# A convolution's running sum moved to PSUM, and two heads' outputs in one staging tile, in a hybrid decoder trunk

## The chip, the cores and the metric

One core of one Trainium2 chip runs the whole program. The metric is the device time of one execution in microseconds.

## The reference, cut to what matters

The program computes DEPTH = 2 layers on x of 1024 tokens by 1024 channels, all in float32:

```python
h = rms_norm(x);  proj = h @ w_in            # one projection, split over three branches
# A) y = a * sigmoid(a_glu); causal depthwise convolution with 31 taps over tokens, 256 channels;
#    layer norm, silu, 256x256 product; times silu(z_conv)
# B) latent attention: 8 heads, key width 96, value width 64, causal softmax in blocks of 128
#    queries; times silu(z_mla)
# C) chunked spatial gating, 256 channels; times silu(z_sg)
x = x + concat(rms_norm(yA), rms_norm(yB), rms_norm(yC)) @ w_out
```

## The kernel before

Every float32 product is made from operands that are split in two parts (a rounded high part and the low rest, both of type fp32r), so a product is two or three matmuls. The high part is a copy on ScalarE (ACT), the low part a subtraction on VectorE (DVE) or GpSimd (POOL). TensorE (PE) has its own order of work, written as a long sequence of units.

A layer runs so. First come the projection units V, A0, A1, U, ZS, ZC, ZM0 and ZM1, eight row tiles or two halves of channels each. A0 and A1 are the two blocks of 128 channels of the convolution branch. When one is projected, its gated input stands in an SBUF tile `yp` (128 channels by 30 + 1024 tokens), and a function `tap(j)` is queued 31 times: tap 0 is a `tensor_scalar` (line 514), taps 1 to 30 are `scalar_tensor_tensor` instructions (line 517), each of which multiplies 1024 shifted columns of `yp` with one weight per channel and adds the running sum `acc`, in place, all in SBUF. The taps of both blocks are handed out as filler work for DVE, 1.45 us apart by the planner's clock (`flow.add_fill`), beside what the projection units ask of DVE: `silu2` (line 549) for ZS, ZC and ZM, `mix` (line 541), and the norm of the gating branch (lines 560 and 565). Behind the taps, four `conv_norm` steps are queued, which transpose `acc` on PE into the bank `ct` (line 596), and from there the branch goes on through `conv_swish` and `conv_point`, all between the matmuls of ZM0 and ZM1. POOL meanwhile makes low parts of weights (line 213) and the products of the gating branch (line 576).

PSUM has eight banks: four of tag `b1` (one bank each, for nearly every output) and two tiles of tag `b2` (two banks each, function `bank2`). The tiles of `b2` hold transposes of the layer's input (`pth`, `pty`) and the scores of attention; nothing asks for one between the end of unit V and the attention.

Attention goes over 8 heads with an order that a greedy planner makes from estimated times: scores (`score`), transposes of the probabilities (`ptrans`), products with the values (`pv`), and `finish`. The values of a head are split by `v_split` into a tile `vh` with the 64 high columns beside the 64 low ones, so one product with the transposed probabilities gives 128 rows, 64 of the high part and 64 of the low. The two are added into a tile `os` of 64 rows by 512 queries (an ACT copy, line 1097, then a DVE addition, line 1098). `finish` transposes `os` back in four pieces of 64 by 128 into a bank `ot` and multiplies the result into the gate tile `zsm` (line 1106). This happens for each head and each half of the queries, 16 times a layer.

The helper `mm` is line 154, every transpose (`tr`) is line 165, and a `split` is lines 169 and 170.

Of the kernel before, what the change touches and what calls it, by code (L numbers as in the profile page):

```python
# [10 lines left out]
F32 = mybir.dt.float32  # L11
# [3 lines left out]
ALU = mybir.AluOpType  # L15
# [4 lines left out]
P = 128  # L20
S = 1024
# [5 lines left out]
TAPS = 31  # L27
# [4 lines left out]
DV = 64  # L32
# [31 lines left out]
for _name, _parts in UNITS:  # L64
# [10 lines left out]
PC_CW, PC_CB, PC_LG, PC_LB, PC_SB, PC_QN, PC_KVN, PC_QG, PC_KG = (  # L75
    0, 62, 64, 66, 68, 72, 78, 80, 81)
# [50 lines left out]
def hybrid_trunk(ctx, tc, x, w, pc, pr, sgw, pww, cst, out):  # L127
    nc = tc.nc
    flow = Flow()

    def open_pool(name, side, bufs=1, **kw):
        cm = tc.tile_pool(name=name, bufs=bufs, side=side, reuse_waits="tile", **kw)
        return cm, cm.__enter__()
# [9 lines left out]
    def bank(name):  # L143
        return ps.tile([P, 512], F32, tag="b1", bufs=4, name=name)
# [218 lines left out]
    for l in range(L):  # L363
# [34 lines left out]
        def chan(un, c0, half, final, name):  # L398

            flow.step()  # L400
            o = bank(name)
            t = hT[half]
            for k in range(KC):
                wh, wl = un.get(k)
                mm3(o, (wh[:, c0:c0 + P], wl[:, c0:c0 + P]), (t[:, 0, k, :], t[:, 1, k, :]),
                    k == 0, k == KC - 1)
                un.used(k, final)
            return o
# [82 lines left out]
        pcs, rg, bgr, dpc = cs  # L491
# [4 lines left out]
        for ct in (0, 1):  # L496
            yp = ap_.tile([P, TAPS - 1 + S], F32, tag="yp", bufs=2, name=f"yp{l}_{ct}")
            nc.gpsimd.memset(yp[:, :TAPS - 1], 0.0)
            un = Unit(l, f"A{ct}")
            for half in (0, 1):  # L500
                g_ps = chan(un, 128, half, False, f"glu{l}_{ct}{half}")
                tg = ap_.tile([P, 512], F32, tag="e2k", bufs=5 - l, name="tg")
                nc.scalar.activation(tg, g_ps, AF.Tanh, scale=0.5)
                a_ps = chan(un, 0, half, half == 1, f"a{l}_{ct}{half}")
                c0 = TAPS - 1 + half * 512
                nc.vector.scalar_tensor_tensor(out=yp[:, c0:c0 + 512], in0=tg, scalar=1.0, in1=a_ps,
                                               op0=ALU.add, op1=ALU.mult)
            acc = ap_.tile([P, S], F32, tag="acc", bufs=2, name=f"acc{l}_{ct}")
            accs.append(acc)

            def tap(j, ct=ct, yp=yp, acc=acc):
                wc = dpc[:, ct * TAPS + j:ct * TAPS + j + 1]
                if j == 0:
                    nc.vector.tensor_scalar(acc, yp[:, 0:S], wc, pcs[:, PC_CB + ct:PC_CB + ct + 1],
                                            op0=ALU.mult, op1=ALU.add)
                else:
                    nc.vector.scalar_tensor_tensor(out=acc, in0=yp[:, j:j + S], scalar=wc, in1=acc,  # L517
                                                   op0=ALU.mult, op1=ALU.add)
            flow.add_fill(1.45, [lambda j=j, f=tap: f(j) for j in range(TAPS)])

# [129 lines left out]
        zsm = cp.tile([P, NT, MW], F32, tag="zsm", name=f"zsm{l}")  # L650
# [6 lines left out]
        for i in range(NT):  # L657
            o = bank(f"pzk{l}_{i}")
# [66 lines left out]
        for half in (0, 1):  # L725
            acc = c2pool.tile([P, 512], F32, tag="sqa", bufs=2, name="sqkv")
            for c in (0, 1):
                o = chan(un, c * P, half, half == 1 and c == 1, f"ckv{l}_{c}{half}")
# [4 lines left out]
        for u in range(3):  # L733
            un = Unit(l, f"CQ{u}")
            for half in (0, 1):
                for c in (0, 1):
                    o = chan(un, c * P, half, half == 1 and c == 1, f"cq{l}_{u}{c}{half}")
# [55 lines left out]
        t1_cm, t1p = open_pool(f"T1_{l}", "left")  # L793
# [74 lines left out]
        def open_t():  # L868
# [3 lines left out]
            t_cm.append(cm)  # L872
            return tp
        attention(nc, flow, t1p, open_t, late_splits, [lambda i=i: query(1, i) for i in range(2, NT)],
                  bank, bank2, mm, mm3, tr, split, split_gain, ident_b, mask_b,
                  ksb, qsb, vsb, zsm, dpc[:DQK, 66:67], (early_load, early_norm), l)
# [101 lines left out]
def attention(nc, flow, t1p, open_t, late_splits, extra, bank, bank2, mm, mm3, tr, split, split_gain, ident_b, mask_b,  # L978
# [1 line left out]

    heads, probs, outs, vhs = {}, {}, {}, {}
    busy = {"act": flow.t, "dve": flow.t}
    LAG = 0.1
    SL_K, SL_S, SL_T, SL_P = 0.0, 0.0, 0.0, 0.0
# [7 lines left out]
    def est(eng, dur, ready):  # L994
        busy[eng] = max(busy[eng], ready + LAG) + dur
        return busy[eng]
# [5 lines left out]
    def v_split(h):  # L1002
        vh = vhs[h] = pool["t"].tile([P, NT, 2, DV], F32R, tag="vh", bufs=2, name=f"vh{l}_{h}")
        hc = vsb[:, :, h * DV:(h + 1) * DV]
        nc.scalar.copy(vh[:, :, 0, :], hc)
        nc.vector.tensor_tensor(out=vh[:, :, 1, :], in0=hc, in1=vh[:, :, 0, :].bitcast(F32),
                                op=ALU.subtract)
        est("dve", 0.6, est("act", 0.55, flow.t))

# [52 lines left out]
    def ptrans(h, half, j):  # L1062
        st = probs[h, half]
        off = max(0, j - 4 * half)
        pt = bank(f"pt{l}_{h}{half}{j}")
        for t in range(off, 4):
            tr(pt[:, t * P:(t + 1) * P], st[t][:, j * P:(j + 1) * P])
        tk = slice(off * P, 512)
        if j == 0:
            sm = st["sum"]  # L1070
            nc.vector.reciprocal(sm[:, 2, :], sm[:, 0, :])  # L1071
            z = zsm[:, half * 4:half * 4 + 4, h * DV:(h + 1) * DV]
            nc.gpsimd.tensor_tensor(out=z, in0=z, in1=sm[:, 2, :].unsqueeze(2).broadcast_to([P, 4, DV]),  # L1073
                                    op=ALU.mult)
        pT = pool["t"].tile([P, 2, 512], F32R, tag="pT", bufs=3, name=f"pT{l}_{h}{half}{j}")
        split(pT[:, 0, tk], pT[:, 1, tk], pt[:, tk])
        n = 512 - off * P
        fh = est("act", n / 1200 + 0.06, flow.t)
        fl = est("dve", n / 960 + 0.08, fh)
        b1_free.remove(min(b1_free))  # L1080
        b1_free.append(fl)
        return pT, tk, max(fh, fl - 0.2)

    def pv(h, half, j, pT, tk):
        nj = 4 * half + 4
        if j == 0:
            outs[h, half] = bank(f"o{l}_{h}{half}")
        o = outs[h, half]
        vv = vhs[h][:, j].rearrange("p a d -> p (a d)")
        mm(o[:, tk], vv, pT[:, 0, tk], j == 0, False)  # L1090
        mm(o[:, tk], vv, pT[:, 1, tk], False, j == nj - 1)
        pt_free.remove(min(pt_free))
        pt_free.append(flow.t)
        if j < nj - 1:
            return None
        os_ = t1p.tile([DV, 512], F32, tag="os", bufs=2, name="os")
        nc.scalar.copy(os_, o[DV:2 * DV, :])
        nc.vector.tensor_tensor(out=os_, in0=o[0:DV, :], in1=os_, op=ALU.add)
        return os_, est("dve", 0.7, est("act", 0.5, flow.t))

    def finish(h, half, os_):
        b = bank(f"ot{l}_{h}{half}")
        for t in range(4):
            tr(b[:, t * DV:(t + 1) * DV], os_[:, t * P:(t + 1) * P])
        z = zsm[:, half * 4:half * 4 + 4, h * DV:(h + 1) * DV]
        nc.vector.tensor_tensor(out=z, in0=b[:, 0:4 * DV].rearrange("p (t d) -> p t d", d=DV), in1=z,
                                op=ALU.mult)
        f = est("dve", 0.35, flow.t)
        b1_free.remove(min(b1_free))
        b1_free.append(f)  # L1110

# [65 lines left out]
    while sq or tq or pq:  # L1177
# [9 lines left out]
        if prio == 3:  # L1187
# [3 lines left out]
            if not x_left:  # L1191
                pool["t"] = open_t()
                v_split(0)
        elif prio == PRIO[0]:
            kind, h, i = sq.pop(0)
            if kind == "load":
                early_load(h)
            elif kind == "s":
                score(h, i)
            elif kind == "v":  # L1200
                v_split(h)
            elif kind == "w":
                splits = splits or late_splits()
                next(splits, None)
            else:
                qk_part(h, kind, i)
        elif prio == PRIO[2]:
            h, half, j = tq.pop(0)
            pT, tk, f = ptrans(h, half, j)
# [3 lines left out]
        else:  # L1213
            _, kind, h, half, *rest = pq.pop(0)
            if kind == "pv":
                j, pT, tk = rest
# [91 lines left out]
```

## Time and profile before

| what | us |
|---|---|
| median of three runs (1318.74, 1319.68, 1321.02) | 1319.68 |
| the profiled execution | 1318.69 |
| its span, first to last instruction | 1316.9 |
| PE busy in the span | 1258.1 |
| DVE busy | 835.6 |
| ACT busy | 532.4 |
| POOL busy | 431.4 |

The profiled execution has 1.8 us around its span, and stands at the lower end of the three runs. Times in the rows below count from the start of the span. Layer 0 has its convolution from about 67 to 220 us and its attention from about 404 to 570 us; layer 1 has the same at about 717 to 870 and 1053 to 1218 us. A busy PE is not PE at its peak, since matmuls are pipelined and a stall inside a queue of matmuls can be shown as busy.

### The profile page before, as it was taken

What the parts mean: (1) busy time and instruction counts of PE and PEld (TensorE: products, weight loads), DVE (VectorE), ACT (ScalarE), POOL (GpSimd) and SP (SyncE); (2) the same over time, 40 slices, a digit from 0 to 9 for tenths busy, and PEclk for the clock granted to TensorE, in tenths of its full rate; (3) what the DMA queues carried; (4) which work ended last, traced back from release to release, by engine and by line L of the source; (5) the groups of instructions that cost most, each with busy time, mean ns of one, the idle gap of its engine ahead of it and who ended that gap; (6) DMA issues with size and microseconds to landing.
All of it is one profiled execution on the core that took longest, in us unless ns stands there. A gap on an engine that the chain in (4) does not pass through costs nothing.

```text
span 1316.9 us, 19326 instructions
## 1 busy us (share of the span) xinstructions
PE 1258.1 (96%) x7566; PEld 1099.6 (84%) x7566; DVE 835.6 (63%) x1337; ACT 532.4 (40%) x1083; POOL 431.4 (33%) x388
## 2 busy tenths in 40 slices
PE   8999969999998999999999997899999989998998
PEld 7889969888996777778898997898889967777886
DVE  7499975114767888763454999631247788887431
ACT  6311324323435777740342122332243477776200
POOL 4733624534573000010046255334436710000100
PEclk9999979999998999999999999899999999999999
DMA  7121212212111000044432112011111100001333
GB/s 284 49 64 33 69 33 65 67 32 72 49 33 33 1 1 1 17 141 125 151 125 64 33 41 92 21 61 48 52 53 49 46 20 1 1 1 29 100 105 104
DMA packets 33820, 77.88 MB, mean 59 GB/s; under 512 B 3777, under 2 KB 12353, under 8 KB 33729
## 3 DMA queue, kind: packets, MB, share of 16 engines
q1 hardware_dynamic: 33728, 76.64, 18.6%
q8 instruction: 60, 0.98, 0.3%
q14 instruction: 32, 0.25, 0.1%
HBM read 64.05 MB, written 12.58 MB: 58 GB/s over the span
## 4 chain that ended last, share of the span: by engine, by line
PE 69%; DVE 21%; ACT 4%; issue 3%; POOL 1%; DMA 0%; SPq 0%; ACTq 0%; DVEq 0%; POOLq 0%
PE po L154 14%; DVE acc L517 13%; PE cq L154 10%; PE s L154 8%; PE qps L154 7%; PE o L154 5%; PE ckv L154 3%; PE pt L165 3%; PE pzk L154 3%; PE ZM L154 3%; PE V L154 2%; PE kps L154 2%; PE vps L154 2%; PE glu L154 2%; PE a L154 2%
## 5 line engine op out<-in xcount | busy, mean ns | idle before, releaser
L213 POOL TENSOR_TENSOR w<-raw,w 128x1024 fp32r<-128x1024 f32 (+1 forms) x49 | 137.2, 2809 | 150.1 <-ACT w L210 96.4
L154 PE MATMUL po<-w,yT 128*128 128x512 f32 x768 | 184.2, 398 | 0.0
L517 DVE SCALAR_TENSOR_TENSOR acc<-yp,dpc,acc 128x1024 f32<-128x1024 f32 x120 | 183.1, 1552 | 1.4
L154 PEld LDWEIGHTS po<-w,yT 128*128 128x128 f32 x768 | 143.0, 188 | 33.3
L154 PE MATMUL s<-kT,qT 96*128 96x384 f32 (+5 forms) x576 | 133.1, 358 | 3.7 <-ACT p L1053 3.7
L154 PE MATMUL o<-pT,vh 128*128 128x512 f32 (+3 forms) x384 | 129.8, 396 | 6.8 <-DVE pT L170 5.6
L154 PE MATMUL cq<-hT,w 128*128 128x512 f32 x576 | 131.9, 390 | 0.0
L154 PEld LDWEIGHTS cq<-hT,w 128*128 128x128 f32 x576 | 107.9, 188 | 22.2
L170 DVE TENSOR_TENSOR pT<-pt,pT 128x512 fp32r<-128x512 f32 x192 | 100.3, 547 | 26.4 <-ACT pT L169 26.0
L154 PEld LDWEIGHTS s<-kT,qT 96*128 96x128 f32 x576 | 95.5, 192 | 17.3 <-ACT p L1053 9.8
L1073 POOL TENSOR_TENSOR zsm<-zsm,rs 128x256 f32<-128x256 f32 x32 | 19.6, 612 | 275.6 <-DVE rs L1071 275.6
L1053 ACT ACTIVATE p<-s,rs 128x128 f32<-128x128 f32 (+7 forms) x128 | 95.0, 742 | 29.7 <-DVE rs L1047 13.0
L169 ACT CAST pT<-pt 128x512 fp32r<-128x512 f32 x192 | 89.0, 480 | 43.4 <-PE pt L165 40.1
L1047 DVE TENSOR_REDUCE rs<-s 128x1 f32<-128x128 f32 (+7 forms) x128 | 95.6, 748 | 15.9 <-PE s L154 15.3
L165 PE MATMUL pt<-cst_sb,p 128*128 128x128 f32 x576 | 94.3, 278 | 10.7 <-DVE qT L170 10.7
L154 PE MATMUL qps<-w,cqT 128*128 128x384 f32 x576 | 102.2, 338 | 0.0
L154 PEld LDWEIGHTS qps<-w,cqT 128*128 128x128 f32 x576 | 100.5, 188 | 0.3
L165 PEld LDWEIGHTS pt<-cst_sb,p 128*128 128x128 f32 x576 | 68.2, 143 | 20.8 <-DVE qT L170 8.6
L154 PEld LDWEIGHTS o<-pT,vh 128*128 128x128 f32 x384 | 65.2, 192 | 17.1 <-DVE pT L170 10.3
L174 DVE SCALAR_TENSOR_TENSOR cqT<-cq,pcs,cqT 128x512 fp32r<-128x512 f32 x24 | 18.0, 749 | 93.9 <-ACT cqT L173 93.9
L210 ACT CAST w<-raw 128x1024 fp32r<-128x1024 f32 (+1 forms) x47 | 49.6, 1057 | 49.9 <-PE a L154 14.9
L154 PE MATMUL ZM<-w,hT 128*128 128x256 f32 x384 | 52.5, 298 | 8.3 <-DVE zc L549 8.3
(318 smaller groups left out, 2269.8 us busy)
## 6 DMA issues: line engine op xcount, KB each, us to landing
raw<-in_w_dram SPq DMA_DIRECT2D x64, 512.0 KB, 3.5
raw<-in_w_dram SPq DMA_DIRECT2D x12, 576.0 KB, 3.7
xt<-in_x_dram SPq DMA_DIRECT2D x8, 512.0 KB, 8.1
xr<-xmid SPq DMA_DIRECT2D x16, 256.0 KB, 2.9
out_dram<-xr SPq DMA_DIRECT2D x16, 256.0 KB, 2.0
yn<-yside SPq DMA_DIRECT2D x24, 128.0 KB, 2.9
yside<-ug SPq DMA_DIRECT2D x8, 256.0 KB, 2.2
yside<-yc SPq DMA_DIRECT2D x8, 256.0 KB, 2.1
```

Of the source, the lines that this page charges most:

```text
L154: nc.tensor.matmul(o, lhsT=lhsT, rhs=rhs, start=start, stop=stop)
L165: nc.tensor.transpose(out=o, in_=in_, identity=ident[:k, :k])
L169: nc.scalar.copy(hi, src)
L170: nc.vector.tensor_tensor(out=lo, in0=src, in1=hi.bitcast(F32), op=ALU.subtract)
L174: nc.vector.scalar_tensor_tensor(out=lo, in0=src, scalar=gain, in1=hi.bitcast(F32), op0=ALU.mult, op1=ALU.subtract)
L210: nc.scalar.copy(wt[:, 0, :sz], raw[:, :sz])
L213: (eng or nc.gpsimd).tensor_tensor(out=wt[:, 1, :sz], in0=raw[:, :sz], in1=wt[:, 0, :sz].bitcast(F32), op=ALU.subtract)
L517: nc.vector.scalar_tensor_tensor(out=acc, in0=yp[:, j:j + S], scalar=wc, in1=acc, op0=ALU.mult, op1=ALU.add)
L1047: nc.vector.tensor_reduce(out=sm[:, 1, t:t + 1], in_=src if nb > 1 else o[:, :wd], axis=AX.XY if nb > 1 else AX.X, op=ALU.max, negate=True)
L1053: nc.scalar.activation(pr_[:, :n].rearrange("p (b n) -> p b n", b=nb), src, AF.Exp, bias=sm[:, 1, t:t + 1], accum_out=sm[:, 0, t:t + 1])
L1073: nc.gpsimd.tensor_tensor(out=z, in0=z, in1=sm[:, 2, :].unsqueeze(2).broadcast_to([P, 4, DV]), op=ALU.mult)
```

## The change

The running sum of the convolution stands in a PSUM tile `run` of tag `b2`, one for each block of channels; taps 0 to 29 write it, taps 1 to 30 read it, and tap 30 writes the SBUF tile `acc`, from which the branch goes on as before. A tap thus has one tensor input in SBUF (`yp`) and one in PSUM, beside its weight, which is one number per partition in SBUF.

In attention, heads are taken in pairs (0 and 1, 2 and 3, ...). An odd head has its high and low value columns swapped in `vh`. The tile `os` has 128 rows; the even head's sum is made in rows 0 to 63, the odd head's in rows 64 to 127, by the same two instructions as before. `finish` runs for odd heads alone: four transposes of 128 by 128, and one multiplication of 512 columns into the gates of both heads. That is 8 times a layer.

```diff
+            run = bank2(f"run{l}_{ct}")
+
+            def tap(j, ct=ct, yp=yp, acc=acc, run=run):
                 wc = dpc[:, ct * TAPS + j:ct * TAPS + j + 1]
                 if j == 0:
-                    nc.vector.tensor_scalar(acc, yp[:, 0:S], wc, pcs[:, PC_CB + ct:PC_CB + ct + 1],
+                    nc.vector.tensor_scalar(run, yp[:, 0:S], wc, pcs[:, PC_CB + ct:PC_CB + ct + 1],
                                             op0=ALU.mult, op1=ALU.add)
                 else:
-                    nc.vector.scalar_tensor_tensor(out=acc, in0=yp[:, j:j + S], scalar=wc, in1=acc,
+                    nc.vector.scalar_tensor_tensor(out=acc if j == TAPS - 1 else run,
+                                                   in0=yp[:, j:j + S], scalar=wc, in1=run,
                                                    op0=ALU.mult, op1=ALU.add)
...
-        nc.scalar.copy(vh[:, :, 0, :], hc)
-        nc.vector.tensor_tensor(out=vh[:, :, 1, :], in0=hc, in1=vh[:, :, 0, :].bitcast(F32),
+        a = h % 2
+        nc.scalar.copy(vh[:, :, a, :], hc)
+        nc.vector.tensor_tensor(out=vh[:, :, 1 - a, :], in0=hc, in1=vh[:, :, a, :].bitcast(F32),
                                 op=ALU.subtract)
...
-        os_ = t1p.tile([DV, 512], F32, tag="os", bufs=2, name="os")
-        nc.scalar.copy(os_, o[DV:2 * DV, :])
-        nc.vector.tensor_tensor(out=os_, in0=o[0:DV, :], in1=os_, op=ALU.add)
-        return os_, est("dve", 0.7, est("act", 0.5, flow.t))
+        if h % 2 == 0:
+            pair_out[half] = t1p.tile([P, 512], F32, tag="os", bufs=2, name="os")
+        os_ = pair_out[half]
+        mine = slice(h % 2 * DV, (h % 2 + 1) * DV)
+        other = slice((1 - h % 2) * DV, (2 - h % 2) * DV)
+        nc.scalar.copy(os_[mine, :], o[other, :])
+        nc.vector.tensor_tensor(out=os_[mine, :], in0=o[mine, :], in1=os_[mine, :], op=ALU.add)
+        f = est("dve", 0.7, est("act", 0.5, flow.t))
+        return (os_, f) if h % 2 else None
 
     def finish(h, half, os_):
         b = bank(f"ot{l}_{h}{half}")
         for t in range(4):
-            tr(b[:, t * DV:(t + 1) * DV], os_[:, t * P:(t + 1) * P])
-        z = zsm[:, half * 4:half * 4 + 4, h * DV:(h + 1) * DV]
-        nc.vector.tensor_tensor(out=z, in0=b[:, 0:4 * DV].rearrange("p (t d) -> p t d", d=DV), in1=z,
-                                op=ALU.mult)
-        f = est("dve", 0.35, flow.t)
+            tr(b[:, t * P:(t + 1) * P], os_[:, t * P:(t + 1) * P])
+        z = zsm[:, half * 4:half * 4 + 4, (h - 1) * DV:(h + 1) * DV]
+        nc.vector.tensor_tensor(out=z, in0=b.rearrange("p (t d) -> p t d", d=P), in1=z, op=ALU.mult)
+        f = est("dve", 0.6, flow.t)
```

## Rows read from the trace of the kernel before

**Rows 1.** The page, part 1: busy us (share of the span) xinstructions.

```profile
PE 1258.1 (96%) x7566; PEld 1099.6 (84%) x7566; DVE 835.6 (63%) x1337; ACT 532.4 (40%) x1083; POOL 431.4 (33%) x388
```

**Rows 2.** The page, part 4: the chain that ended last, by line.

```profile
PE po L154 14%; DVE acc L517 13%; PE cq L154 10%; PE s L154 8%; PE qps L154 7%; PE o L154 5%; PE ckv L154 3%; PE pt L165 3%; PE pzk L154 3%; PE ZM L154 3%; PE V L154 2%; PE kps L154 2%; PE vps L154 2%; PE glu L154 2%; PE a L154 2%
```

**Rows 3.** The waits of PE, whole span: us in total, times, longest us.

```profile
PE ct L165 <- DVE acc L517: 12.3, 2, 6.3
...
PE ZM L154 <- DVE zc L549: 8.3, 2, 4.3
```

**Rows 4.** Timeline of PE, layer 0: start us, us, instructions [idle before <-releaser].

```profile
160.58 5.92 PE L154 MATMUL ZM<-w,hT 128*128 128x256 f32 x48
166.34 0.27 PE L165 MATMUL ct<-cst_sb,acc 128*128 128x128 f32 x1
170.65 1.01 PE L154 MATMUL ZM<-w,hT 128*128 128x256 f32 x3 [4.04 <-DVE zc L549]
177.60 0.90 PE L165 MATMUL ct<-cst_sb,acc 128*128 128x128 f32 x3 [5.94 <-DVE acc L517]
178.15 7.54 PE L154 MATMUL ZM<-w,hT 128*128 128x256 f32 x45
```

**Rows 5.** The timeline of PE at the same place in layer 1.

```profile
827.53 7.17 PE L154 MATMUL ZM<-w,hT 128*128 128x256 f32 x45
```

**Rows 6.** Windows: stretch, length, PE, PEld, DVE, ACT, POOL busy; PEclk, DMA.

```profile
178.00:186.00 8.00, 8.00 (x53) 8.00 (x52) 2.28 (x8) 0.27 (x1) 0.69 (x1) 0.72 0.01 2
```

**Rows 7.** Timelines of ACT and DVE where PE waits, layer 0.

```profile
161.36 0.59 ACT L548 ACTIVATE tz<-ZC 128x512 f32<-128x512 f32 x1
...
175.67 0.68 DVE L549 SCALAR_TENSOR_TENSOR zc<-tz,ZC 128x512 f32<-128x512 f32 x1
176.26 1.28 DVE L517 SCALAR_TENSOR_TENSOR acc<-yp,dpc,acc 128x1024 f32<-128x1024 f32 x1
```

**Rows 8.** Line 517 by itself: count, duration ns min/median/max, first and last start.

```profile
L517 DVE SCALAR_TENSOR_TENSOR acc<-yp,dpc,acc x120: 1268/1277/3785, 68.8 to 825.6; 128x1024 f32<-128x1024 f32 x120
```

**Rows 9.** Groups of DVE, 67 to 178.2 us: busy us, mean ns | idle before.

```profile
L517 DVE SCALAR_TENSOR_TENSOR acc<-yp,dpc,acc 128x1024 f32<-128x1024 f32 x60 | 91.4, 1550 | 0.7
...
L514 DVE TENSOR_SCALAR acc<-yp,dpc,pcs 128x1024 f32<-128x1024 f32 x2 | 1.6, 808 | 0.0
```

**Rows 10.** Timeline of DVE and POOL, 111 to 125 us.

```profile
112.62 10.33 POOL L213 TENSOR_TENSOR w<-raw,w 128x1024 fp32r<-128x1024 f32 x2 [18.62 <-PE mix L154]
117.27 1.39 DVE L541 SCALAR_TENSOR_TENSOR ug<-mix,pcs,ug 128x512 f32<-128x512 f32 x2
118.59 5.45 DVE L517 SCALAR_TENSOR_TENSOR acc<-yp,dpc,acc 128x1024 f32<-128x1024 f32 x2
```

**Rows 11.** Groups of DVE by shape, whole span: busy us, mean ns | idle before.

```profile
L854 DVE SCALAR_TENSOR_TENSOR yn<-zsm,yst,bgr 128x512 f32<-128x512 f32 x12 | 8.8, 745 | 2.2 <-POOL yst L178 2.2
...
L541 DVE SCALAR_TENSOR_TENSOR ug<-mix,pcs,ug 128x512 f32<-128x512 f32 x8 | 5.7, 736 | 0.0
```

**Rows 12.** Timeline of PE in attention, layer 0: a return transpose, then probability transposes.

```profile
425.82 0.23 PE L154 MATMUL s<-mask_b,ident_b 128*128 128x128 bf16 x1
425.98 0.46 PE L165 MATMUL ot<-cst_sb,os 64*128 64x64 f32 x4
426.37 0.74 PE L154 MATMUL o<-pT,vh 128*128 128x512 f32 x2
...
428.86 0.23 PE L154 MATMUL s<-mask_b,ident_b 128*128 128x128 bf16 x1
428.93 0.50 PE L165 MATMUL pt<-cst_sb,p 128*128 128x128 f32 x3
429.19 0.48 PE L154 MATMUL o<-pT,vh 128*128 128x512 f32 x1
```

**Rows 13.** Windows in attention, columns as above.

```profile
440.00:460.00 20.00, 19.38 (x130) 15.54 (x127) 16.24 (x31) 15.22 (x36) 1.23 (x2) 1.00 0.01 1
```

**Rows 14.** Timeline of PE in the output projection of layer 0.

```profile
602.62 37.76 PE L154 MATMUL po<-w,yT 128*128 128x512 f32 x161
```

More of the change, by code (lines that the diff above doesn't have):

```diff
@@ L509, in hybrid_trunk @@
             accs.append(acc)
-            def tap(j, ct=ct, yp=yp, acc=acc):
+            run = bank2(f"run{l}_{ct}")
+            def tap(j, ct=ct, yp=yp, acc=acc, run=run):
                 wc = dpc[:, ct * TAPS + j:ct * TAPS + j + 1]
                 if j == 0:
-                    nc.vector.tensor_scalar(acc, yp[:, 0:S], wc, pcs[:, PC_CB + ct:PC_CB + ct + 1],
+                    nc.vector.tensor_scalar(run, yp[:, 0:S], wc, pcs[:, PC_CB + ct:PC_CB + ct + 1],
                                             op0=ALU.mult, op1=ALU.add)
                 else:
-                    nc.vector.scalar_tensor_tensor(out=acc, in0=yp[:, j:j + S], scalar=wc, in1=acc,
+                    nc.vector.scalar_tensor_tensor(out=acc if j == TAPS - 1 else run,
+                                                   in0=yp[:, j:j + S], scalar=wc, in1=run,
                                                    op0=ALU.mult, op1=ALU.add)
@@ L979, in attention @@
               ksb, qsb, vsb, zsm, kgain, early, l):
-    heads, probs, outs, vhs = {}, {}, {}, {}
+    heads, probs, outs, vhs, pair_out = {}, {}, {}, {}, {}
     busy = {"act": flow.t, "dve": flow.t}
```

## The prediction

> **What bounds the kernel now.** I read the page's busy times first. PE is busy for 96% of the span, DVE for 63% [rows 1]: the kernel is bound by TensorE, and an edit to DVE's work can pay only in stretches where PE stands still for DVE. The chain that ended last shows that such stretches exist: its second entry, 13%, is DVE at line 517, the taps of the convolution [rows 2]. A chain's share is no gain, since most of that time PE works beside the taps; what a stall costs is read from the waits of PE. There, two waits of the convolution stage, one of each kind in a layer, add up to 12.3 and 8.3 us: `ct`, the transposes of the finished sum, for the last tap, and ZM for the `silu2` of ZC, whose bank it needs [rows 3]. The timeline gives the place: after 48 matmuls of ZM and one transpose at 166.34 us, PE stands until 170.65, issues three matmuls, and stands again until 177.60 [rows 4].
>
> Both waits have one cause, that DVE is late. ScalarE had the tanh of the last ZC pair ready at 161.36 + 0.59 = 161.95 us, and DVE comes to it at 175.67, 13.7 us later; the last tap runs from 176.26 to 177.54 [rows 7]. So the next question is why the taps are late. Half of the 120 taps take 1277 ns or less, but the slowest takes 3785 [rows 8], and over the 60 of layer 0 the mean is 1550 [rows 9]. The timeline of DVE and POOL shows the pair that quarrels: two of POOL's weight subtractions span 112.62 to 122.95, and two taps that begin at 118.59 take 5.45 us instead of 2.5 [rows 10].
>
> **The change, part by part: the taps.** Only taps 1 to 30 have two tensors in SBUF now. Does taking one to PSUM end the quarrel? The trace has the same instruction in the new form, line 541: one tensor in PSUM, one in SBUF, a weight per partition. Two of them run at 117.27, inside POOL's 10.33 us, in 1.39 us together [rows 10], and the mean of all eight is 736 ns [rows 11]; none is stretched. I take it that the new taps aren't either. [...]
>
> What does a tap cost without the quarrel? The PSUM input is free by the nearest rows: 736 ns for 512 columns with an input in PSUM, 745 with both in SBUF [rows 11]. The PSUM output is shown nowhere: DVE writes no PSUM in this kernel. Its low end is nothing: between lines 854 and 517, 512 columns more cost 1277 - 745 = 532 ns, 1.04 ns each, and no row with two tensor inputs goes below that, so I exclude a gain. Its high end is that reading and writing the same bank share its time, one more pass over the 1024 columns, 2 x 532 ns: a tap would take 2341 ns. What speaks for the low end is that PE adds into a PSUM bank, which is a read and a write, at 37.76 us / 161 / 512 = 0.46 ns a column [rows 14], faster than a tap's 1.04 ns. I take nothing.
>
> So a layer's taps lose 60 x (1550 - 1277) ns = 16.4 us. The first taps lose something: 808 ns for 1024 columns [rows 9] is 0.79 ns a column, which I expect to go to a tap's 1277 when the output is in PSUM, 2 x 0.47 = 0.9 us. DVE would finish the last tap at 177.54 - 16.4 + 0.9 = 162.0 us. It can't quite: its order has the last ZC pair ahead of that tap, ready at 161.95, so 161.95 + 0.68 + 1.28 = 163.9. PE comes to `ct` at 166.34, 2.4 us later: both waits vanish whole, **20.6 us** over two layers [rows 3]. The spare time is also what hides the unknown: 60 taps could each cost some 70 ns more ((166.34 - 162.0) / 60) before PE waits again.
>
> [...]
>
> With the stall goes what follows it. [...] 48 matmuls of ZM take 5.92 us at full clock, so 45 take 5.55; after the stall they took 7.54 and 7.17 [rows 4, 5]: 1.99 + 1.62 = **3.6 us**. What is late next is the norm behind `ct`, which PE meets again 5.5 us later; DVE and POOL need some 3 us for it, and have nothing else queued then.
>
> POOL's subtractions, no longer held up by taps, end earlier; nobody on PE waited for them here, so I count nothing. The two `b2` tiles that `run` takes have no other user between V and attention, so nothing waits for them.
>
> **The heads in pairs.** Per pair of heads and half, four transposes of 64 rows go, and one multiplication. The copies, additions and value splits stay as many and as large. An `os` tile now lives for two heads instead of one, but a pair asks for it a whole half of a head after the last pair's transposes have read it, and the norm behind head 7 already waited for that head's `finish`, so I count nothing there. From the score matmul ahead of it to the next product, a return transpose costs PE 0.16 + 0.39 us; three transposes of 128 rows cost 0.07 + 0.26, so four about 0.07 + 0.35 [rows 12]. A pair pays 1.10 now and 0.42 then: 0.68 us, and 16 pairs in two layers 10.9. If the longer approach (0.16) belongs to something else, it is 2 x 0.39 - 0.35 = 0.43, or 6.9. In attention PE is busy 19.38 of 20 us with DVE at 16.24 and ACT at 15.22 [rows 13], so most of this counts; but a faster PE meets waits that are hidden now, and the greedy planner's order shifts with it. Low end nothing, high end 10.9; I take a little under the lower price, **6.5 us**.
>
> Sum: 20.6 + 3.6 + 6.5 = 30.7 us from the profiled execution's 1318.69 gives 1288.0. That execution stands 1.0 us under the median of the runs shown, which I leave inside the range.
>
> **The rivals.** *Dearer PSUM writes, in part.* If a tap costs 100 to 250 ns more than 1277, DVE ends at 168 to 177 us and PE stalls for a part: at 150 ns more, 162.0 + 9.0 = 171.0, a stall of about 5 us a layer with about half of the slow clock. Saved: 10.6 + 1.8 + 6.5 = 18.9, time 1300. For it: no row shows the write. Against: rows 14.
>
> *The taps still meet POOL,* because the weight is an SBUF operand as well. Then only attention gains: 1312, or 1318 when its waits take that too. Against: line 541, which has such a weight.
>
> *Slower than before.* Reading and writing one bank cost two passes: 2341 ns a tap. From a mean of 1550 on DVE is as late as now, and with attention's 6.5 us the line is at 1550 + 6.5 / 120 x 1000 = 1604. At 2341 each layer is later by 60 x 0.79 = 47 us: 1318.7 + 95 - 6.5 = 1407. Against: rows 14 again.
>
> *Attention gives nothing or loses.* PE's order changes and it waits for DVE or ACT instead: 1294 at no gain, 1300 if some 3 us a layer are lost. For it: 3% of PE's time there is idle already.
>
> **How the numbers follow.** My forecast, both waits gone and attention between 0 and 10.9 us better, 0.70 (1283 to 1295); dearer writes in part 0.10; taps still meeting POOL 0.07, of which 0.03 land within 0.2%; two passes 0.06; attention at a loss 0.07. The range, 1281 to 1303, holds the first, the last and the better half of the second, less the tails. A measurement of this kernel can tell about 0.2%, 2.6 us, from no change. Faster 0.90, the same 0.03, slower 0.07 (two passes, and one part in a hundred for mishaps of attention with the taps unhelped).
>
> **What would show it.** Right: taps of 1.25 to 1.35 us with no slow ones beside POOL; no wait of PE at `ct` or at ZM for `zc`; granted clock 1.00 through that stage; 64 return transposes of 128 rows, and attention of each layer 3 to 5 us shorter. Wrong: taps all longer than 1.35 us, a wait of PE at another line of ZM, `cb` or `cy`, or an attention with more waits of PE for `pT` than now.

## The result, and the profile after

The changed kernel takes 1283.44 us, the median of four runs (1283.21 to 1284.51), against 1319.96 for the kernel before: a ratio of 0.9725, 95% interval 0.9708 to 0.9742. The profiled execution takes 1283.21 us with a span of 1281.2, 35.5 us less than before. The forecast was 1288.0 with a range of 1281 to 1303.

The page's busy times, and the chain that ended last, by line:

```profile
PE 1244.0 (97%) x7502; PEld 1091.0 (85%) x7502; DVE 797.0 (62%) x1321; ACT 531.7 (42%) x1083; POOL 397.9 (31%) x388
...
PE po L154 14%; PE cq L154 10%; PE s L154 8%; PE qps L154 7%; PE o L154 5%; PE pt L165 4%; PE ZC L154 4%; PE U L154 4%; PE ZS L154 4%; PE ZM L154 4%; PE ckv L154 3%; PE glu L154 3%; PE a L154 3%; PE pzk L154 3%; PE V L154 2%; PE kps L154 2%
```

DVE lost 38.6 us of busy time and POOL, which the change doesn't touch, 33.5. PE's busy time fell by 14.1 of the 35.7 us of span; the rest had been idle time of PE. The taps, 13% of the chain before [rows 2], are gone from it, and the units U, ZS and ZC that ran beside them stand in their place. The waits of PE, longest in total first (us in total, times, longest):

```profile
PE pt L165 <- DVE qT L170: 10.3, 12, 4.2
PE o L154 <- DVE pT L170: 5.9, 14, 0.6
PE s L154 <- ACT p L1059: 3.4, 9, 0.9
PE ot L165 <- DVE os L1108: 2.8, 2, 1.4
```

These are the first four lines; neither `ct` nor ZM is anywhere in the list [rows 3]. The timeline of PE at the place of the stall in layer 0:

```profile
160.66 5.92 PE L154 MATMUL ZM<-w,hT 128*128 128x256 f32 x48
166.42 0.27 PE L165 MATMUL ct<-cst_sb,acc 128*128 128x128 f32 x1
166.45 2.28 PE L154 MATMUL ZM<-w,hT 128*128 128x256 f32 x17
168.57 0.49 PE L165 MATMUL ct<-cst_sb,acc 128*128 128x128 f32 x3
168.81 3.96 PE L154 MATMUL ZM<-w,hT 128*128 128x256 f32 x31
```

PE comes to `ct` within 0.1 us of the time before and goes on [rows 4]. Fourteen more ZM matmuls now stand between the first transpose and the next three: the order of instructions on each engine is made when the program is built, from estimated times, and has moved a little. The granted clock, in the windows of [rows 6] and the one ahead of it:

```profile
166.00:178.00 12.00, 12.00 (x103) 12.00 (x103) 6.71 (x18) 3.75 (x7) 2.39 (x3) 1.00 0.25 83
178.00:186.00 8.00, 8.00 (x70) 8.00 (x70) 4.55 (x11) 4.17 (x10) 2.85 (x2) 1.00 0.01 2
```

It is 1.00 in both; it was 0.62 in the first and 0.72 in the second. And the taps by themselves (duration ns min/median/max; line 520 is taps 1 to 30, line 517 tap 0):

```profile
L520 DVE SCALAR_TENSOR_TENSOR run<-yp,dpc,run x116: 1275/1290/1290, 69.4 to 793.6; 128x1024 f32<-128x1024 f32 x116
L517 DVE TENSOR_SCALAR run<-yp,dpc,pcs x4: 1341/1346/1349, 68.0 to 721.9; 128x1024 f32<-128x1024 f32 x4
L520 DVE SCALAR_TENSOR_TENSOR acc<-yp,dpc,run x4: 1266/1276/1281, 134.0 to 794.9; 128x1024 f32<-128x1024 f32 x4
```

The slowest of taps 1 to 30 takes 1290 ns where it took 3785 [rows 8]. Before, every one of the nine slow taps of a layer (2.1 to 3.8 us) overlapped a POOL instruction that reads SBUF; now no tap is stretched beside POOL. The two engines at 112 to 119 us, where they met in [rows 10]:

```profile
112.69 4.79 POOL L213 TENSOR_TENSOR w<-raw,w 128x1024 fp32r<-128x1024 f32 x2 [20.15 <-PE mix L154]
...
113.80 1.28 DVE L520 SCALAR_TENSOR_TENSOR run<-yp,dpc,run 128x1024 f32<-128x1024 f32 x1
...
115.66 2.47 DVE L520 SCALAR_TENSOR_TENSOR run<-yp,dpc,run 128x1024 f32<-128x1024 f32 x2
```

Two subtractions take 4.79 us and not 10.33, and two taps beside them 2.47 and not 5.45 [rows 10]. DVE at the end of the taps:

```profile
162.06 0.69 DVE L553 SCALAR_TENSOR_TENSOR zc<-tz,ZC 128x512 f32<-128x512 f32 x1 [0.47 <-ACT tz L552]
162.67 1.28 DVE L520 SCALAR_TENSOR_TENSOR run<-yp,dpc,run 128x1024 f32<-128x1024 f32 x1
163.99 1.28 DVE L520 SCALAR_TENSOR_TENSOR acc<-yp,dpc,run 128x1024 f32<-128x1024 f32 x1
```

DVE waits for the last ZC pair, where it came 13.7 us late, and ends the last tap at 165.27, 1.2 us ahead of PE's first transpose at 166.42. In attention, the return transposes of a pair of heads:

```profile
433.15 0.60 PE L165 MATMUL ot<-cst_sb,os 128*128 128x128 f32 x4
433.51 0.48 PE L154 MATMUL o<-pT,vh 128*128 128x512 f32 x1
```

From the first of its transposes to the next product it takes 0.36 us, against 0.39 before [rows 12], when four transposes served one head and not two.

By PE's own marks, from the first ZM matmul of a layer to its first `pzk`, the stage is 42.11 us before and 29.11 after in layer 0, 42.00 and 29.11 in layer 1: **25.9 us** less. From the first score to the first matmul of the output projection it is 187.27 and 182.12, 186.64 and 181.97: **9.8 us** less. The other stages moved by less than 0.2 us in sum.

### The profile page after: what moved, and what is told of

It is laid out like the page before. It is cut to its first block, busy times and chain, and to the rows that moved or that the text cites. A ratio compares the mean times of both kernels' runs of the same rounds, so it can differ in the third digit from the quotient of the medians.

```text
span 1281.2 us, 19181 instructions
## 1 busy us (share of the span) xinstructions
PE 1244.0 (97%) x7502; PEld 1091.0 (85%) x7502; DVE 797.0 (62%) x1321; ACT 531.7 (42%) x1083; POOL 397.9 (31%) x388
## 4 chain that ended last, share of the span: by engine, by line
PE 87%; DVE 5%; ACT 5%; issue 1%; POOL 1%; DMA 0%; SPq 0%; ACTq 0%; POOLq 0%; DVEq 0%
PE po L154 14%; PE cq L154 10%; PE s L154 8%; PE qps L154 7%; PE o L154 5%; PE pt L165 4%; PE ZC L154 4%; PE U L154 4%; PE ZS L154 4%; PE ZM L154 4%; PE ckv L154 3%; PE glu L154 3%; PE a L154 3%; PE pzk L154 3%; PE V L154 2%; PE kps L154 2%
## 5 line engine op out<-in xcount | busy, mean ns | idle before, releaser
L213 POOL TENSOR_TENSOR w<-raw,w 128x1024 fp32r<-128x1024 f32 (+1 forms) x49 | 118.4, 2423 | 181.1 <-ACT w L210 113.5
L520 DVE SCALAR_TENSOR_TENSOR run<-yp,dpc,run 128x1024 f32<-128x1024 f32 x116 | 145.4, 1286 | 1.4
L154 PEld LDWEIGHTS s<-kT,qT 96*128 96x128 f32 x576 | 96.4, 193 | 14.1 <-ACT p L1059 6.6
L165 PE MATMUL pt<-cst_sb,p 128*128 128x128 f32 x576 | 95.6, 280 | 10.3 <-DVE qT L170 10.3
L1053 DVE TENSOR_REDUCE rs<-s 128x1 f32<-128x128 f32 (+7 forms) x128 | 95.8, 749 | 14.1 <-PE s L154 13.5
L918 DVE TENSOR_TENSOR xr<-po,xr 128x512 f32<-128x512 f32 x24 | 16.6, 691 | 65.6 <-PE po L154 65.6
```

Of the source, the lines that this page charges most:

```text
L154: nc.tensor.matmul(o, lhsT=lhsT, rhs=rhs, start=start, stop=stop)
L165: nc.tensor.transpose(out=o, in_=in_, identity=ident[:k, :k])
L213: (eng or nc.gpsimd).tensor_tensor(out=wt[:, 1, :sz], in0=raw[:, :sz], in1=wt[:, 0, :sz].bitcast(F32), op=ALU.subtract)
L520: nc.vector.scalar_tensor_tensor(out=acc if j == TAPS - 1 else run, in0=yp[:, j:j + S], scalar=wc, in1=run, op0=ALU.mult, op1=ALU.add)
L918: nc.vector.tensor_tensor(out=xr, in0=o, in1=xr, op=ALU.add)
L1053: nc.vector.tensor_reduce(out=sm[:, 1, t:t + 1], in_=src if nb > 1 else o[:, :wd], axis=AX.XY if nb > 1 else AX.X, op=ALU.max, negate=True)
```

## The experiments

**The taps alone.** The first hunk of the diff, on the kernel before.

> Only the running sum in PSUM, attention as before. If the two parts are independent, as the two traces read (conv stage 12.99 and 12.90 us shorter, attention 5.16 and 4.68 us): 1319 - 25.9 = 1293 us, taps of 1.29 us, no wait of PE at ct or at ZM. Rival, the gain of attention came from a better order behind a shorter conv stage: attention is shorter here too and the time is 1284 to 1289.

Measured: 1293.43 us, ratio 0.9799 (0.9784 to 0.9813); conv stage 13.0 and 12.9 us shorter, attention as before. The longest wait of PE is now that of attention, and `ct` and ZM are not among its waits:

```profile
PE pt L165 <- DVE qT L170: 10.7, 14, 4.2
```

**The heads alone.** All other hunks, on the kernel before.

> Only the heads in pairs, taps as before in SBUF. Independent parts: 1319 - 9.8 = 1309 us, with the two stalls of some 10 us a layer still there. Rival as for the taps alone: 1314 to 1319.

Measured: 1309.58 us, ratio 0.992 (0.9904 to 0.9937); span 1307.6, 9.3 us less. Both stalls are there, as the waits of PE show:

```profile
PE ct L165 <- DVE acc L517: 11.9, 2, 5.9
...
PE ZM L154 <- DVE zc L549: 8.3, 2, 4.3
```

The two parts nearly add up: the spans are 25.9 and 9.3 us shorter, 35.2 in sum, where both together gave 35.7. By PE's marks attention is 5.2 and 4.6 us shorter in the two layers, as much as in the changed kernel; what is missing lies in the convolution stage of layer 1, which is 0.8 us longer here. The rival, that attention gains from a shorter convolution stage ahead of it, fell.

**POOL that only writes.** Does PSUM matter at all, or only that POOL's reads don't meet the taps? Here POOL fills the low parts of the weights of five units and of CKV with zeros, which reads nothing; the kernel thus leaves these low parts out of its products:

```diff
-        (eng or nc.gpsimd).tensor_tensor(out=wt[:, 1, :sz], in0=raw[:, :sz],
-                                         in1=wt[:, 0, :sz].bitcast(F32), op=ALU.subtract)
+        if PIECES[n % NP][0] in ("U", "ZS", "ZC", "ZM0", "ZM1", "CKV"):
+            nc.gpsimd.memset(wt[:, 1, :sz].bitcast(F32), 0.0)
+        else:
+            (eng or nc.gpsimd).tensor_tensor(...)
```

> The kernel before, taps in SBUF. GpSimd's subtractions that make the low part of the weights of U, ZS, ZC, ZM and CKV are replaced by a fill with zeros, which writes SBUF and reads none of it; the products lose that low part. If the slow taps come from GpSimd's reads beside them, 7 of the 9 slow taps of a layer go (two stand beside the gating products and may stay), the mean tap falls from 1.55 to about 1.3 us, the stall at ct and ZM is under 2 us a layer, and the time is 1293 to 1297 us, without any PSUM. Rival, the taps gained by what PSUM itself does or by the changed order of instructions: the mean tap stays at 1.5 or more and the time at 1315 to 1319.

Measured: 1291.71 us, ratio 0.9783 (0.9763 to 0.9802), just below what I expected, with the sums in SBUF. The taps (the file's lines are moved by three), and one place where POOL's fills meet them:

```profile
L520 DVE SCALAR_TENSOR_TENSOR acc<-yp,dpc,acc x120: 1267/1277/2316, 68.7 to 799.2; 128x1024 f32<-128x1024 f32 x120
```

```profile
110.59 2.47 DVE L520 SCALAR_TENSOR_TENSOR acc<-yp,dpc,acc 128x1024 f32<-128x1024 f32 x2
...
111.52 1.85 POOL L214 MEMSET w<- 128x1024 f32 x2 [21.68 <-PE U L154]
```

The fills in the stretch of the taps take 0.95 to 1.07 us each, and no tap beside them is slow. One slow tap of 2.3 us a layer is left of nine, beside a gating product of POOL, which reads. PE doesn't wait at `ct` or ZM. So the gain of the taps is that of the quarrel ended; what PSUM gives is a way to end it that leaves nothing out. Unit ZM1 is also 1.1 us shorter in each layer, and the output projection of layer 0 is 1.5 us longer, so the small difference in time from the taps alone says nothing.

**One block of the two.** How does the stall follow DVE's lateness? First, block 0 alone in PSUM.

```diff
-            run = bank2(f"run{l}_{ct}")
+            run = bank2(f"run{l}_{ct}") if ct == 0 else acc
```

> The running sum in PSUM for the first block of 128 channels alone; the second keeps its sum in SBUF; attention as before. The slow taps of the first block (three before the second block starts, and some of those that alternate, about 7.5 us of the 16.4 excess) go. If PE's stall is DVE's lateness and nothing else, it shrinks from 10 to 2 or 3 us a layer and the time is 1298 to 1306 us. Rival, the place of ct in PE's order decides and not DVE's lateness: the stall is gone whole or stays whole, 1293 or 1319.

Measured: 1321.21 us, ratio 1.0006 (0.9996 to 1.0016): nothing gained. My expectation failed, and the rival, that the place of `ct` decides, seemed to win. The durations say otherwise. No tap of block 0 is slow, and those of block 1 still are:

```profile
L520 DVE SCALAR_TENSOR_TENSOR acc<-yp,dpc,acc x60: 1266/1282/3626, 115.8 to 828.6; 128x1024 f32<-128x1024 f32 x60
L520 DVE SCALAR_TENSOR_TENSOR run<-yp,dpc,run x58: 1280/1290/1291, 68.9 to 757.3; 128x1024 f32<-128x1024 f32 x58
```

What changed is DVE's order. Before, the blocks' taps alternate from 95 us on; here block 0 goes first to its end, and block 1 begins only then, behind `mix`. DVE's timeline, there and at the last tap:

```profile
109.25 1.28 DVE L520 SCALAR_TENSOR_TENSOR acc<-yp,dpc,run 128x1024 f32<-128x1024 f32 x1
112.69 0.75 DVE L545 SCALAR_TENSOR_TENSOR ug<-mix,pcs,ug 128x512 f32<-128x512 f32 x1 [2.16 <-ACT ug L534]
113.35 1.84 DVE L517 TENSOR_SCALAR acc<-yp,dpc,pcs 128x1024 f32<-128x1024 f32 x1
...
179.27 1.28 DVE L520 SCALAR_TENSOR_TENSOR acc<-yp,dpc,acc 128x1024 f32<-128x1024 f32 x1
```

The last tap ends at 180.55 us, 3.0 later than before, and PE waits for it until 180.60. The slow taps' excess fell from 16.4 to 30 x (1604 - 1277) ns = 9.8 us, and more than that came back: from 67 us to its last tap DVE is idle 7.0 us and not 1.0; 15 taps of block 0 follow one another 1.32 us apart, where alternating ones start every 1.20; the first tap of block 1 takes 1842 ns. The order on PE has moved as well: 48 ZM matmuls and not three stand between the first transpose and the next, so the lateness is paid at three places:

```profile
PE ct L165 <- DVE acc L520: 8.2, 2, 5.4
PE cb L165 <- DVE nt L606: 6.5, 2, 3.3
PE ZM L154 <- DVE zc L553: 6.0, 2, 3.0
```

That is 20.7 us where it was 20.6 at two [rows 3]. PE's order changed and the sum of its waits stayed, and its wait at `ct` ends with DVE's last tap. So the time that the rival named came out, but by DVE's lateness and not by the place of `ct`. It is my price of DVE's end that had left out the order.

**The other block,** with the same line for `ct == 1`. Here the order stays alternating.

> The running sum in PSUM for the second block of 128 channels alone, where DVE's order of the two blocks stays alternating as in the kernel before. In that kernel five slow taps of layer 0 with 9.9 us of excess belong to the second block, four with 6.4 us to the first. If PE's stall is DVE's lateness and the lateness is the sum of the excess, the last tap ends at 177.5 - 9.9 + 0.5 = 168.1 us, the stall falls from 10 to 1 or 2 us a layer, and the time is 1295 to 1300 us. Rival, as the first block alone showed, half of the taps is worth nothing: the stall stays at 8 us or more and the time at 1316 to 1321 us.

Measured: 1301.23 us, ratio 0.9858 (0.9839 to 0.9878), just above what I expected. DVE's last tap of layer 0, and a wait of PE that is new:

```profile
167.05 1.27 DVE L520 SCALAR_TENSOR_TENSOR acc<-yp,dpc,run 128x1024 f32<-128x1024 f32 x1
```

```profile
121.12 0.50 PE L154 MATMUL mix<-vn,sgs 128*128 128x512 f32 x1 [1.89 <-DVE ug L545]
```

The last tap ends at 168.32, where 168.1 was forecast from the sum of the excess, and PE doesn't wait for it at all: it comes to `ct` only at 169.44, 3.1 us later than before. Of these, 1.0 us had been there since unit V, ahead of any tap, and 1.9 are the wait at `mix` for DVE, which is late there by the slow taps of block 0. So one block's taps in PSUM are worth 19 of the 27 us of both when the order stays, and part of the rest is paid at another place.

**Transposes of 128 rows, still one head each.** Is a return transpose dear by its number or by its 64 rows? On the kernel before, rows 64 to 127 are filled with zeros, and all 128 are transposed:

```diff
-        os_ = t1p.tile([DV, 512], F32, tag="os", bufs=2, name="os")
+        os_ = t1p.tile([P, 512], F32, tag="os", bufs=2, name="os")
+        nc.gpsimd.memset(os_[DV:2 * DV, :], 0.0)
...
-            tr(b[:, t * DV:(t + 1) * DV], os_[:, t * P:(t + 1) * P])
+            tr(b[:, t * P:(t + 1) * P], os_[:, t * P:(t + 1) * P])
```

> The kernel before with 16 finishes a layer as before, one head each, but each transposes four pieces of 128 rows by 128 (the lower 64 rows are zeros that GpSimd fills in) instead of 64 by 64. As many transposes as before, twice the columns. If a return transpose is dear because TensorE changes to 64 rows and back, a finish falls from 0.55 to 0.42 us: 32 x 0.13 = 4.2 us, attention 2.1 us a layer shorter, 1314 to 1316 us. Rival, its price is the number of transposes and their columns: a finish grows by about 0.1 us, attention 1 to 2 us a layer longer, 1322 to 1324 us; then the saving of the pairs comes from their number alone.

Measured: 1315.65 us, ratio 0.9967 (0.9955 to 0.998): twice the columns, and faster. The timeline of PE around one of them:

```profile
425.55 0.23 PE L154 MATMUL s<-mask_b,ident_b 128*128 128x128 bf16 x1
425.62 0.61 PE L165 MATMUL ot<-cst_sb,os 128*128 128x128 f32 x4
425.98 0.71 PE L154 MATMUL o<-pT,vh 128*128 128x512 f32 x2
```

0.07 us from the score matmul and 0.36 to the next product, against 0.16 and 0.39 [rows 12]: 0.43 us, as priced. By PE's marks attention is 2.1 us shorter in layer 0, as expected, but only 0.8 in layer 1; its waits grew a little (`ot` for `os` from 2.8 to 3.1 us), and the rest of that difference is open. So some 3 of the heads' 9.8 us come from the shape, and the rest from there being half as many. Why TensorE takes longer with 64 rows than with 128 is not shown.

**A step further: the next quarrel for POOL.** The longest wait of PE that is left is for `qT` at the start of attention, 4.2 us a layer. POOL's timeline in the changed kernel, layer 0:

```profile
385.36 3.57 POOL L246 TENSOR_TENSOR w<-raw,w 128x256 fp32r<-128x256 f32 x4
388.89 0.62 POOL L817 TENSOR_TENSOR t<-qsb,tab 128x64 f32<-128x64 f32 x2
389.47 2.96 POOL L246 TENSOR_TENSOR w<-raw,w 128x256 fp32r<-128x256 f32 x4
392.39 1.00 POOL L178 TENSOR_TENSOR qs<-qs,mhalf 128x4 f32<-128x4 f32 x1
```

Low parts of the output weights (line 246), wanted some 165 us later, stand in POOL's queue ahead of the rotation (line 817) of the last query tile but one and the scale (line 178) of the last. The edit ties them to head 1, by a factor of 1.0 that is made from one of its sums:

```diff
-            nc.vector.tensor_copy(wt[:, 0, :sz], raw[:, :sz])
+            nc.vector.tensor_scalar(wt[:, 0, :sz], raw[:, :sz], gate, None, op0=ALU.mult)
...
-                splits = splits or late_splits()
+                if splits is None:
+                    gate = t1p.tile([P, 1], F32, tag="gate", name=f"gate{l}")
+                    nc.vector.tensor_scalar(gate, probs[h, 0]["sum"][:, 1, 0:1], 0.0, 1.0,
+                                            op0=ALU.mult, op1=ALU.add)
+                    splits = late_splits(gate)
```

> The changed kernel, with one edit beside it: at the start of attention GpSimd's quarter subtractions for the output weights (line 246) stand ahead of the rotation of the last two query tiles, and PE waits 4.2 us a layer for what comes of it, with 6.8 us at half clock behind. Here the high part of these weights is multiplied by a 1.0 that is made from head 1's first score, so that none of this can be placed ahead of head 1. If the same quarrel is at work there, the wait of PE for qT falls from 4.2 to under 1.5 us a layer, the half clock goes, and the time is 1270 to 1278 us. Rival, the wait is that of the last query's own chain: it stays at 3 us or more, or moves to DVE, and the time is 1281 to 1287 us.

Measured: 1278.31 us, ratio 0.9685 (0.967 to 0.9699), clear of the changed kernel's interval and the fastest here, 0.3 us above what I expected. POOL's timeline of the same steps, and the waits of PE:

```profile
388.94 1.01 POOL L178 TENSOR_TENSOR qs<-qs,mhalf 128x4 f32<-128x4 f32 x1 [1.19 <-DVE qs L808]
390.62 0.61 POOL L817 TENSOR_TENSOR t<-qsb,tab 128x64 f32<-128x64 f32 x2 [0.67 <-DVE qsb L814]
```

```profile
PE pt L165 <- DVE qT L170: 3.8, 12, 0.9
...
PE pt L165 <- DVE kT L174: 2.0, 2, 1.0
```

The last scale is 3.45 us earlier, though this run's attention starts 1.0 us later, and the wait falls from 4.2 to 0.9 us, with a new one of 1.0 for `kT` right behind it. The slow clock goes in part only: in 390 to 400 us it is 0.83 against 0.75. I had called it the same quarrel, and it isn't: none of these instructions is stretched to three times its length as the taps were (line 246 takes 720 to 1185 ns in the changed kernel); most of the time went by the place in POOL's queue, where line 817 stands behind 3.57 us of subtractions and line 178 behind 2.96.

## Why the prediction was right, point by point

**The cause of the stall** was as argued: DVE was late because taps with two SBUF tensors met POOL's reads. This is shown from both sides, by taking the taps' second tensor out of SBUF and by taking POOL's reads away: from the first ZM matmul to the first `pzk` either run takes 29.1 us in each layer, where it was 42.

**The price of a tap.** Forecast 1277 ns, measured 1286 in the mean and at most 1290: the unknown PSUM output costs 9 ns, and a tap that reads and writes the same PSUM tile stays far from the 2341 ns of two passes. The low end was right, and with it the rivals of dearer writes fell, in part and in whole; so did the one that the weight would keep up the quarrel. A PSUM input costs nothing that shows: line 545, the old 541, has 744 ns with one, and line 858, the old 854, 747 with both inputs in SBUF. The first taps were forecast at 1277 and take 1346 ns, without effect.

**DVE's end** was forecast at 163.9 and is 165.27; PE's margin of 2.4 us came out as 1.2. Most of the difference is in the order: two taps stand behind the last ZC pair, not one. Both waits vanished whole, 20.6 us, as forecast.

**The slow clock** was mis-sized: 3.6 us forecast. The stage gained 25.9, so 5.3 remain beside the waits. I had priced the 45 ZM matmuls alone; the three before them and the three transposes were slow too, with a granted clock of 0.50 in 170 to 172 and in 176 to 180 us. The transposes took 0.90 us [rows 4] and take 0.49 now, 0.8 us over two layers; the three matmuls took 1.01 and 0.62 us, where three at full clock take 0.37 (3 x 5.92 / 48 [rows 4], at a granted clock of 1.00), 0.9 us in sum. That is the missing 1.7.

**The heads** were mis-sized too, and this is the larger part of the 4.8 us by which the profiled execution came out below the forecast: 6.5 forecast, 9.8 measured. The working had 10.9 as its upper price, from 0.55 us for four transposes of 64 rows and 0.42 for four of 128. The step that failed is where I chose: I put the longer approach of 0.16 us down as perhaps another's, and took a little under the lower price for waits that a faster PE would meet. The approach is the transposes' own, as the run with 128 rows shows (0.07 at the same place). And PE met few new waits: those of attention are 10.3, 5.9, 3.4 and 2.8 us now, and were 10.7, 5.6, 3.7 and 2.8. Of the 1.1 us that are missing to 10.9, about 1.0 lies in four of the 16 sets of return transposes, which take 0.60 us to the next product and not 0.36; why is not shown.

## What to carry to other kernels

When a queue of equal instructions has a median of 1277 ns and a maximum of 3785, look at what the other engine on the same memory does at the slow ones, before counting instructions; the cheapest cure may be to move one operand, and the trace may have an instruction that is already in the new form, as line 541 was here. What such a cure is worth is read at the wait of the engine that bounds the kernel, and only as much as the late engine comes earlier there: one block of the two moved gave 19 us of 27 in one order of instructions and nothing in another. A transpose of fewer rows among matmuls of 128 can cost more than a full one: here four of 64 rows took 0.55 us and four of 128 took 0.43.

## What the runs showed of the hardware that I had not expected

Taps that add to the same sum one after the other start every 1.32 us; taps of two sums in turn start every 1.20, in SBUF and in PSUM alike. In the changed kernel the last two taps of block 1 start at 162.67 and 163.99 us, and these 16 are of two sums in turn:

```profile
92.27 19.16 DVE L520 SCALAR_TENSOR_TENSOR run<-yp,dpc,run 128x1024 f32<-128x1024 f32 x16
```

I read the 0.12 us as the price of an instruction that needs the one just before it; no run tests that by itself. The contention goes both ways: while taps with two SBUF tensors followed one another without a gap, two subtractions of POOL took 10.33 us [rows 10], and beside PSUM taps the same two take 4.79. POOL's eight gating products take 2.27 us each beside taps in SBUF, also where the taps themselves aren't slow, and 1.30 beside taps in PSUM. And `tensor_scalar` loses more than taps 1 to 30 by going to PSUM: 808 ns [rows 9] became 1346, where theirs went from 1277 to 1286.
